# Order of the mixer's projections, gates and recurrence end in a two-layer block: attention's projection ahead of the recurrence's end, the inverse's matrices four turns behind their load

## The chip, the cores and the metric

The kernel runs on 1 core of one Trainium2 chip. The metric is the device time of one execution in microseconds, the median of several; lower is better. TensorE (PE) multiplies matrices, VectorE (DVE), ScalarE (ACT) and GpSimd (POOL) work elementwise, and SyncE (SP) issues the DMAs. Each engine carries out its own list of instructions in the order in which the program was built, and waits at an instruction until what that one needs is there.

## The reference, cut to what matters

Two layers (`DEPTH = 2`) over 256 tokens of width 1024, in float32. Each is a feed-forward block, a mixer and a second feed-forward block, all with norms before and behind and a residual.

```python
m = _mixer(h, w_in[l], rwkv_params, diff_params, w_branch[l], w_out[l], lambda_init)
x = x + _rms_norm(m, mix_norm_post[l])

def _mixer(h, w_in, rwkv_params, diff_params, w_branch, w_out, lambda_init):
    z = h @ w_in
    z_dsa, z_rwkv, z_diff, z_gate = jnp.split(z, GROUP_CUTS, axis=-1)
    y_a = _dsa_branch(z_dsa)                     # attention over the 64 best keys
    y_b = _rwkv7_branch(z_rwkv, *rwkv_params)    # a recurrence over the tokens
    y_c = _diff_branch(z_diff, *diff_params, lambda_init)   # differential attention
    branches = jnp.stack([y_a, y_b, y_c], axis=2)
    proj = jnp.einsum('blnc,ncd->blnd', branches, w_branch)
    gates = jax.nn.sigmoid(z_gate.reshape(B, L, N_BRANCH, D_MODEL))
    merged = jnp.sum(gates * proj, axis=2)
    return merged @ w_out
```

So three branches a, b and c (n = 0, 1, 2), each 512 wide, are projected to 1024, gated, summed and multiplied by `w_out`.

## The kernel before

**Large products.** Each weight matrix comes in raw tiles of 1 MB (`raw`, issued by SP at L201, two places), is split into a high part `wh` (ACT, a cast, L220) and a rest `wl` (DVE, and while `self.share` is on sometimes POOL, L220), and each 128x512 product is three matmuls (L229 to L231: `wh` with the low part of the data, `wh` with the high part, `wl` with the high part). There are four places for `wh`/`wl`; a pool `extra` opens more of them where other tiles have gone. A raw place is free when both splits have read it, and only then does SP issue the next load into it.

**The mixer** (L469 to L615) runs the large products of the weights `w_in` (queries, keys, values, gates), then three projections with `w_branch` (`proj_steps`, L576) and then `w_out`. Beside these stand three jobs, written as generators: `dsa` (branch a), `rwkv_in` with `rwkv_solve` and `rwkv` (branch b) and `diff` (branch c). Each step of a large product calls `tick()`, which advances the jobs by one `yield`. What a job issues is put in at high priority, but its PE instructions stand behind the large product's last matmul at that time; instructions of the other engines are not bound to that. A priority list then sets one order for each engine, at build time.

**The gates.** `gate_steps(n, h)` (L505) computes half h of gate n and copies it to a tile (L509). Gate 1 lies in the tiles `g1`, in the pool `tp`; half 0 of gate 0 lies in `g0`, in the place of a residual tile; the rest in the pool `ep`. Order: (1,0), (1,1), (0,0), (0,1), (2,1); (2,0) was computed earlier. The sigmoids of all gates (L599 to L601) come behind everything, and exponentials (L629, of the softmax) use another table of ACT functions.

**The recurrence.** `rwkv_solve` writes matrices to DRAM and reads them back in another layout (`d` L990 and L995, `zs` L992, `xs` L997), yields once (L1001), builds the matrices `Z` of an inverse from `zs` on DVE (L1004) and `T` from `xs` on POOL (L1008), and then runs a chain of small products (`Z,up`; `W,T`). `rwkv` ends with `yb` (L1176). The mixer drains this job (L564), closes the pools of the recurrence (`c1`, L565), opens the pool `gp` in their place (L566) and splits `yb` into `yh`, `yl` (L571 to L574).

**The end of the mixer.** Projection 1 (of `yb`), projection 0 (of `ya`, adds projection 1's gated result), then the pools `c2` (with `tp`) are closed and the pool `extra` with seven places is opened over them (L608, L609); projection 2 adds projection 0's result, its sum is transposed (L587), split into `mh`, `ml`, and multiplied by `w_out` together with it in one run of steps (L610 to L615). For the first 128 tokens (t = 0) `w_out` runs ahead of the second (t = 1). `post_norm` (squares L309, rstd L311 and L312, L367, L368), the next block's norm (L332) and the transposes of `xn` (L341) follow; then the feed-forward block starts with `hl`, `hh`.

Of the kernel before, what the change touches and what calls it, by code (L numbers as in the profile page):

```python
# [11 lines left out]
AF = mybir.ActivationFunctionType  # L12
# [11 lines left out]
LAG = 2  # L24
# [13 lines left out]
class Block:  # L38
# [430 lines left out]
    def mixer(self, l, ctx):  # L469
        nc, ins = self.nc, self.ins  # L470
# [7 lines left out]
        acc = lambda: self.bank(self.acc)  # L478
# [3 lines left out]
        def rows(c0):  # L482
            return lambda k0, k: w[k0 * 128:(k0 + k) * 128, c0:c0 + 512]
# [9 lines left out]
        gates, mx, kept = {}, {}, {}  # L493

        def gate(n, t, h):

            if n != 1 and (n, h) != (0, 0):
                return self.ep.tile([128, 512], F32, name="g", tag="s")
            key, o = (n, t if n == 1 else 0), h if n == 1 else t
            if not o:  # L500
                kept[key] = (self.tp.tile([128, 1024], F32, name="g1", tag="qk", bufs=4) if n == 1 else
                             self.xp.tile([128, 1024], F32, name="g0", tag="x0"))
            return kept[key][:, o * 512:o * 512 + 512]

        def gate_steps(n, h, acc=acc):  # L505
            def gate_done(t, ps):
                with self.pe():
                    gates[n, t, h] = gate(n, t, h)
                    nc.scalar.copy(gates[n, t, h], ps[0])  # L509

            return self.steps_b(rows(C_G + n * D + h * 512), 512, 8, self.hx, acc, gate_done)
# [11 lines left out]
        c1 = ExitStack()  # L523
# [15 lines left out]
            return d  # L539

        self.gp = None
        st = {}
        self.share = SHARE
        st["qi"] = cols(C_QI, "qi")
        raw = self.load_a(w, C_KI, 72)
# [6 lines left out]
        rwkv = self.rwkv_in(w, l, st)  # L552
# [5 lines left out]
            self.tick()  # L558
        st["dk"] = cols(C_DK, "dk")
        diff = self.start(self.diff(st, vd))  # L560
        for n, h in ((1, 0), (1, 1), (0, 0), (0, 1), (2, 1)):
            self.run_skew(gate_steps(n, h))
        self.share = 0
        self.drain(rwkv)  # L564
        c1.__exit__(None, None, None)  # L565
        self.gp = self.pool(ctx, "gp", side="right")  # L566

        def pieces(y):
            return lambda k, t: tuple(p[k // 2][:, k % 2, t * 128:t * 128 + 128] for p in y)

        yb = self.new_y(self.gp)  # L571
        with self.p1():
            for i in range(2):
                self.split_to(yb[0][i], yb[1][i], st["yb"][:, 2 * i:2 * i + 2, :])  # L574

        def proj_steps(n, y, prev=None, last=False, acc=acc):  # L576
            def proj_done(h):
# [17 lines left out]
                out += self.steps_b(src, 512, 4, pieces(y), acc, proj_done(h))  # L595
            return out

        self.drain(dsa, diff)
        with self.p1(), self.behind(self.exp):  # L599
            for g in gates.values():  # L600
                nc.scalar.activation(g, g, AF.Sigmoid)  # L601
        self.run_skew(proj_steps(1, yb))
        self.run_skew(proj_steps(0, st["ya"], prev=1))
        for t in range(2):
            self.x[t] = self.xp.tile([128, D], F32, name=f"xr{t}", tag=f"x{t}")
            nc.sync.dma_start(self.x[t], xd[t])
        gpost = self.bcast(ins["mix_norm_post"][l], D, self.gbp, "gb", "gpost")
        c2.__exit__(None, None, None)  # L608
        self.extra = self.pool(ctx, "extra", EXTRA)  # L609
        steps = proj_steps(2, st["yc"], prev=0, last=True, acc=self.wide)  # L610
        wo = ins["w_out"][l]
        steps += self.steps_b(lambda k0, k: wo[k0 * 128:(k0 + k) * 128, :], D, 8,
                              lambda k, t: tuple(p[:, k % 4, :] for p in mx[t, k // 4]), self.wide,
# [176 lines left out]
    def rwkv_in(self, w, l, st):  # L790

        nc = self.nc

        def shifted(dst, m0):
            raw = self.load_a(w, C_RW + m0 * 128, 256)
            ps = self.bank(self.acc)
            self.gemm_a(raw, 256, ps)
            with self.pe():
                for j in range(2):
                    z, p = dst[j], ps[:, j * T:(j + 1) * T]  # L800
                    nc.scalar.mul(z, p, self.omu[:, m0 + j:m0 + j + 1])
                    nc.vector.scalar_tensor_tensor(z[:, 1:T], p[:, 0:T - 1], self.mu[:, m0 + j:m0 + j + 1], z[:, 1:T],
                                                   op0=OP.mult, op1=OP.add)

        wa = self.rs.tile([128, T], F32, name="wa", bufs=1)
        sg = self.rs.tile([128, T], F32, name="sg", bufs=1)
        shifted([wa, sg], 12)
        strip = self.rs.tile([128, 16, 16], F32, name="strip", tag="q", bufs=8)
        halves = [dict(hf=hf, sg=sg) for hf in range(2)]
        self.start(self.rwkv_lora(halves, wa, sg))  # L810
        for hf, h in enumerate(halves):
            for n, m0 in (("k", 4), ("v", 8), ("r", 0)):
                d = self.ep.tile([128, 2, T], F32, name=n, tag="s")
                shifted([d[:, 0, :], d[:, 1, :]], m0 + 2 * hf)
                h[n] = d
            if hf == 0:
                self.start(self.rwkv_pre(h, strip))

        def job():
            yield from self.rwkv_pre(halves[1], strip)  # L820
            while "ready" not in halves[0]:
                yield
            Z = yield from self.rwkv_solve(list(zip(halves[0]["up"], halves[1]["up"])), strip)
            yield from self.rwkv(halves, Z, l, st)

        return self.start(job())

    def rwkv_lora(self, halves, wa, sg):
# [140 lines left out]
    def rwkv_solve(self, Ls, strip):  # L969

        nc = self.nc
# [26 lines left out]
        d16 = self.diag16.rearrange("p (b x) -> p b x", x=16)[:, None, :, :].to_broadcast([128, 4, 8, 16])  # L998
        even = self.even.rearrange("p b h x -> p (b h) x")[:, None].to_broadcast([128, 4, 8, 16])
        Zs, Ts = [], []  # L1000
        yield  # L1001
        for q in range(4):
            Zs.append(self.ep.tile([128, 4, 128], F32, name="Z", tag="s"))
            nc.vector.tensor_tensor(Zs[q].rearrange("p u (g x) -> p u g x", x=16),  # L1004
# [8 lines left out]
        for i, mask in enumerate(self.lev):  # L1013
# [23 lines left out]
            for g in range(2):  # L1037
                yield

                m = 64 if i == 2 else 128  # L1040
# [200 lines left out]
```

## Time and profile before

| | us |
|---|---|
| time, median of 3 runs (1476.93 to 1480.19) | 1479.91 |
| the profiled execution, device time | 1478.08 |
| its span in the profile | 1476.4 |
| PE busy (97% of the span) | 1430.3 |
| DVE busy (62%) | 910.1 |
| ACT busy (48%) | 707.7 |
| POOL busy (11%) | 166.5 |

PE is busy for all but 46 us of the span, so a change moves the time by what it adds to or takes from PE's idle time and PE's half clock; what other engines do counts where PE waits for it. The mixer of layer 0 ends at about 548 us of the span, that of layer 1 some 728 us later, with the same instructions. Idle times in square brackets in the rows are those of the row's engine just before the instruction, with what released it.

### The profile page before, as it was taken

The page shows a single profiled execution, that of the slowest core. Times are in us where ns is not written, and L with a number is a line of the kernel's source. Part 1 is how long each engine was busy: PE and PEld are TensorE (multiplying, and loading weights), DVE is VectorE, ACT ScalarE, POOL GpSimd, SP SyncE. Part 2 cuts the span into 40 slices and gives each one's busy share as a digit, 9 for nine tenths or more (in the row PEclk, how much of TensorE's full clock was granted, in tenths as well). Part 3 has the DMA queues.
Part 4 walks back from the last instruction along what each step waited for, and adds up shares of the span by engine and source line. Part 5 has one row for each costly group of instructions (what it writes and reads, how often), then busy time and mean ns, then how long its engine had stood idle before and what let it go on. Part 6 is the DMA issues. An engine that isn't in the chain of part 4 may idle for free.

```text
span 1476.4 us, 22534 instructions
## 1 busy us (share of the span) xinstructions
PE 1430.3 (97%) x9229; PEld 1277.5 (87%) x9229; DVE 910.1 (62%) x1312; ACT 707.7 (48%) x1086; POOL 166.5 (11%) x132
## 2 busy tenths in 40 slices
PE   8999999999799999999999999999889999999997
PEld 5999879988688778998889998799778888799986
DVE  5555463898655776555565554558976567755543
ACT  5444455555463454444454444455544544544442
POOL 1000011332212000000000000213421110000000
PEclk9999999999899999999999999999999999999999
DMA  6656656444433464665646556554442425555653
GB/s 219 194 173 206 208 201 183 141 143 130 119 97 104 157 229 143 191 194 188 226 144 190 182 200 230 169 172 149 139 130 89 141 87 205 179 171 173 209 176 113
DMA packets 176415, 247.05 MB, mean 167 GB/s; under 512 B 17908, under 2 KB 128440, under 8 KB 176312
## 3 DMA queue, kind: packets, MB, share of 16 engines
q1 hardware_dynamic: 176312, 245.62, 51.4%
q8 instruction: 72, 1.18, 0.3%
q14 instruction: 31, 0.25, 0.0%
HBM read 241.80 MB, written 3.80 MB: 166 GB/s over the span
## 4 chain that ended last, share of the span: by engine, by line
PE 78%; DVE 12%; DMA 4%; ACT 3%; issue 2%; POOL 0%; DVEq 0%; POOLq 0%; ACTq 0%; SPq 0%
PE ps L229 12%; PE ps L231 12%; PE ps L230 12%; PE ps L225 11%; PE ps L226 11%; PE ps L227 11%; PE ps L188 7%; DVE wl L220 3%; DMA raw<-in_w_out_dram 1%; ACT wh L220 1%; DVE sc L670 1%; PE ps L341 1%; DMA raw<-in_w_in_dram 1%; DVE sc L665 1%; DMA raw<-in_ffn_w_gate_dram 1%
## 5 line engine op out<-in xcount | busy, mean ns | idle before, releaser
L220 DVE TENSOR_TENSOR wl<-raw,wh 128x1024 fp32r<-128x1024 f32 x398 | 491.7, 1243 | 383.9 <-ACT wh L220 381.8
L220 ACT CAST wh<-raw 128x1024 fp32r<-128x1024 f32 x438 | 453.1, 1046 | 504.9 <-PE ps L226 232.0
L225 PE MATMUL ps<-hl,wh 128*128 128x256 f32 (+1 forms) x1712 | 488.9, 286 | 0.0
L226 PE MATMUL ps<-hh,wh 128*128 128x256 f32 (+1 forms) x1712 | 486.2, 284 | 0.0
L227 PE MATMUL ps<-hh,wl 128*128 128x256 f32 (+1 forms) x1712 | 486.0, 284 | 0.0
L225 PEld LDWEIGHTS ps<-hl,wh 128*128 128x128 f32 (+1 forms) x1712 | 327.0, 191 | 2.2 <-issue 1.3
L226 PEld LDWEIGHTS ps<-hh,wh 128*128 128x128 f32 (+1 forms) x1712 | 327.1, 191 | 0.4
L227 PEld LDWEIGHTS ps<-hh,wl 128*128 128x128 f32 (+1 forms) x1712 | 327.1, 191 | 0.0
L229 PE MATMUL ps<-wh,hl 128*128 128x512 f32 x384 | 161.0, 419 | 2.2 <-DVE hl L220 1.9
L231 PE MATMUL ps<-wl,hh 128*128 128x512 f32 x384 | 152.6, 398 | 2.4 <-DVE wl L220 2.4
L230 PE MATMUL ps<-wh,hh 128*128 128x512 f32 x384 | 151.6, 395 | 0.0
L229 PE MATMUL ps<-wh,gl 128*128 128x512 f32 x352 | 138.7, 394 | 0.0
L231 PE MATMUL ps<-wl,gh 128*128 128x512 f32 x352 | 138.4, 393 | 0.0
L230 PE MATMUL ps<-wh,gh 128*128 128x512 f32 x352 | 138.4, 393 | 0.0
L220 POOL TENSOR_TENSOR wl<-raw,wh 128x1024 fp32r<-128x1024 f32 x40 | 99.5, 2486 | 250.3 <-ACT wh L220 177.5
L312 POOL TENSOR_TENSOR rstd<-rstd,mhalf 128x1 f32<-128x1 f32 x24 | 20.2, 843 | 904.3 <-DVE rstd L311 904.3
L231 PEld LDWEIGHTS ps<-wl,hh 128*128 128x128 f32 x384 | 72.6, 189 | 22.1 <-DVE wl L220 5.1
L229 PEld LDWEIGHTS ps<-wh,hl 128*128 128x128 f32 x384 | 72.9, 190 | 20.1 <-issue 3.8
L230 PEld LDWEIGHTS ps<-wh,hh 128*128 128x128 f32 x384 | 73.0, 190 | 13.0
L231 PEld LDWEIGHTS ps<-wl,gh 128*128 128x128 f32 x352 | 66.0, 188 | 15.5
L230 PEld LDWEIGHTS ps<-wh,gh 128*128 128x128 f32 x352 | 66.0, 188 | 15.2
L229 PEld LDWEIGHTS ps<-wh,gl 128*128 128x128 f32 x352 | 66.0, 188 | 15.1
(267 smaller groups left out, 1481.2 us busy)
## 6 DMA issues: line engine op xcount, KB each, us to landing
raw<-in_w_in_dram SPq DMA_DIRECT2D x66, 1024.0 KB, 5.1
raw<-in_ffn_w_up_dram SPq DMA_DIRECT2D x44, 1024.0 KB, 5.3
raw<-in_ffn_w_down_dram SPq DMA_DIRECT2D x44, 1024.0 KB, 4.9
raw<-in_ffn_w_gate_dram SPq DMA_DIRECT2D x43, 1024.0 KB, 5.3
raw<-in_w_branch_dram SPq DMA_DIRECT2D x12, 1024.0 KB, 5.0
raw<-in_w_out_dram SPq DMA_DIRECT2D x8, 1024.0 KB, 5.8
gpre<-in_ffn_norm_pre_dram SPq DMA_DIRECT2D x4, 512.0 KB, 5.3
gpost<-in_ffn_norm_post_dram SPq DMA_DIRECT2D x4, 512.0 KB, 6.2
```

The costliest lines, as they stand in the source:

```text
L188: self.small = self.nc.tensor.matmul(*a, **k)
L220: return self.nc.scalar.copy(hi, src), (engine or self.nc.vector).tensor_sub(lo, src, hi.bitcast(F32))
L225: mm(ps, wh, xl, start=first, stop=False)
L226: mm(ps, wh, xh, start=False, stop=False)
L227: self.last = mm(ps, wl, xh, start=False, stop=last)
L229: mm(ps, xl, wh, start=first, stop=False)
L230: mm(ps, xh, wh, start=False, stop=False)
L231: self.last = mm(ps, xh, wl, start=False, stop=last)
L312: nc.gpsimd.tensor_tensor(r, r, self.mhalf[:, 0:1], op=OP.pow)
L341: self.tr = nc.tensor.transpose(ps[:, k, :], xns[h][:, k * 128:(k + 1) * 128], self.ident)
L665: nc.vector.scalar_tensor_tensor(sc, rl[:, j, :], wi[:, t, head:head + 1], src, op0=OP.mult, op1=OP.add)
L670: nc.vector.match_replace(sc, m8, sc, USED)
```

## The change

Two things change, each in both layers.

First, the mixer's order. Gates come as (0,0), (0,1), (1,0), (1,1), (2,1); the sigmoids of gate 0 are issued after (1,0), those of gates 1 and 2 behind the recurrence's end. Projection 0 (of `ya`) stands ahead of that end and adds nothing; the recurrence's own job calls `close()`, which closes its pools, opens `gp` and splits `yb`. Then projection 1 adds projection 0's result, and projection 2 adds projection 1's, so that the `g1` tiles in the pool `tp` are read until projection 2's last addition, while the pool `extra` is opened over them as before.

Second, `rwkv_solve` yields 2 * LAG = 4 times instead of once between the loads `zs`, `xs` and the building of `Z` and `T`.

```diff
--- before.py
+++ after.py
@@ -539,7 +539,16 @@
             return d
 
         self.gp = None
-        st = {}
+
+        def close():
+
+            c1.__exit__(None, None, None)
+            self.gp = self.pool(ctx, "gp", side="right")
+            y = st["ybs"] = self.new_y(self.gp)
+            for i in range(2):
+                self.split_to(y[0][i], y[1][i], st["yb"][:, 2 * i:2 * i + 2, :])
+
+        st = {"close": close}
         self.share = SHARE
         st["qi"] = cols(C_QI, "qi")
         raw = self.load_a(w, C_KI, 72)
@@ -558,20 +567,8 @@
             self.tick()
         st["dk"] = cols(C_DK, "dk")
         diff = self.start(self.diff(st, vd))
-        for n, h in ((1, 0), (1, 1), (0, 0), (0, 1), (2, 1)):
-            self.run_skew(gate_steps(n, h))
-        self.share = 0
-        self.drain(rwkv)
-        c1.__exit__(None, None, None)
-        self.gp = self.pool(ctx, "gp", side="right")
-
         def pieces(y):
             return lambda k, t: tuple(p[k // 2][:, k % 2, t * 128:t * 128 + 128] for p in y)
-
-        yb = self.new_y(self.gp)
-        with self.p1():
-            for i in range(2):
-                self.split_to(yb[0][i], yb[1][i], st["yb"][:, 2 * i:2 * i + 2, :])
 
         def proj_steps(n, y, prev=None, last=False, acc=acc):
             def proj_done(h):
@@ -595,19 +592,31 @@
                 out += self.steps_b(src, 512, 4, pieces(y), acc, proj_done(h))
             return out
 
+        def open_gates(n):
+            for (m, t, h), g in gates.items():
+                if m == n:
+                    nc.scalar.activation(g, g, AF.Sigmoid)
+
+        for n, h in ((0, 0), (0, 1), (1, 0), (1, 1), (2, 1)):
+            self.run_skew(gate_steps(n, h))
+            if (n, h) == (1, 0):
+                with self.p1():
+                    open_gates(0)
+        self.run_skew(proj_steps(0, st["ya"]))
+        self.share = 0
+        self.drain(rwkv)
+        with self.p1(), self.behind(self.exp):
+            for n in (1, 2):
+                open_gates(n)
+        self.run_skew(proj_steps(1, st["ybs"], prev=0))
         self.drain(dsa, diff)
-        with self.p1(), self.behind(self.exp):
-            for g in gates.values():
-                nc.scalar.activation(g, g, AF.Sigmoid)
-        self.run_skew(proj_steps(1, yb))
-        self.run_skew(proj_steps(0, st["ya"], prev=1))
         for t in range(2):
             self.x[t] = self.xp.tile([128, D], F32, name=f"xr{t}", tag=f"x{t}")
             nc.sync.dma_start(self.x[t], xd[t])
         gpost = self.bcast(ins["mix_norm_post"][l], D, self.gbp, "gb", "gpost")
         c2.__exit__(None, None, None)
         self.extra = self.pool(ctx, "extra", EXTRA)
-        steps = proj_steps(2, st["yc"], prev=0, last=True, acc=self.wide)
+        steps = proj_steps(2, st["yc"], prev=1, last=True, acc=self.wide)
         wo = ins["w_out"][l]
         steps += self.steps_b(lambda k0, k: wo[k0 * 128:(k0 + k) * 128, :], D, 8,
                               lambda k, t: tuple(p[:, k % 4, :] for p in mx[t, k // 4]), self.wide,
@@ -822,6 +831,7 @@
                 yield
             Z = yield from self.rwkv_solve(list(zip(halves[0]["up"], halves[1]["up"])), strip)
             yield from self.rwkv(halves, Z, l, st)
+            st["close"]()
 
         return self.start(job())
 
@@ -998,7 +1008,8 @@
         d16 = self.diag16.rearrange("p (b x) -> p b x", x=16)[:, None, :, :].to_broadcast([128, 4, 8, 16])
         even = self.even.rearrange("p b h x -> p (b h) x")[:, None].to_broadcast([128, 4, 8, 16])
         Zs, Ts = [], []
-        yield
+        for _ in range(2 * LAG):
+            yield
         for q in range(4):
             Zs.append(self.ep.tile([128, 4, 128], F32, name="Z", tag="s"))
             nc.vector.tensor_tensor(Zs[q].rearrange("p u (g x) -> p u g x", x=16),
```

What this does to the order of the engines' instructions, in layer 0 (layer 1 reads alike). In a row, `wl<-raw,wh` is the second split of a weight, `yl<-ps,yh` that of `ya` or `yc`, and a wait for a DMAHW queue is one for a transfer.

**DVE, where `Z` is built.** Before:

```order
L988 COPY XT<-X 128x256 [waits DVE_49]
L220 TENSOR_TENSOR wl<-raw,wh 128x1024 [waits DMAHW1_49,PE_49,Activation_49]
L220 TENSOR_TENSOR yl<-ps,yh 128x512 [waits Activation_49]
L1004 TENSOR_TENSOR Z<-zs,blk_1947 128x512 [waits DMAHW5_49]
L1004 TENSOR_TENSOR Z<-zs,blk_1947 128x512 x2
L220 TENSOR_TENSOR wl<-raw,wh 128x1024 [waits DMAHW2_49,PE_49,Activation_49]
L220 TENSOR_TENSOR yl<-ps,yh 128x512 [waits Activation_49]
L1004 TENSOR_TENSOR Z<-zs,blk_1947 128x512
```

After:

```order
L998 COPY XT<-X 128x256 [waits DVE_49]
L220 TENSOR_TENSOR wl<-raw,wh 128x1024 [waits DMAHW1_49,PE_49,Activation_49]
L220 TENSOR_TENSOR yl<-ps,yh 128x512 [waits Activation_49]
L1015 TENSOR_TENSOR Z<-zs,blk_1947 128x512 [waits DMAHW5_49]
L1015 TENSOR_TENSOR Z<-zs,blk_1947 128x512 x2
L220 TENSOR_TENSOR wl<-raw,wh 128x1024 [waits DMAHW2_49,PE_49,Activation_49]
L220 TENSOR_TENSOR yl<-ps,yh 128x512 [waits Activation_49]
L1015 TENSOR_TENSOR Z<-zs,blk_1947 128x512
```

Nothing moved: three of the four `Z` stand ahead of the same `wl` and the same `yl` (the split of `ya`, which empties the PSUM bank that the next product `dk,dq` on PE is written to). What moved is PE's `Z,up`, from 6 matmuls behind the products `dk,dq` to 28 behind.

**PE, at the recurrence's end** (`yc` and `yt` are its last transposes; L229 with `yl` opens a projection). Before:

```order
L191 MATMUL ps<-ident,yc 128x128 [waits DVE_49]
L191 MATMUL ps<-ident,yc 128x128 x2
L191 MATMUL ps<-ident,yt 128x128 x8
L229 MATMUL ps<-wh,yl 128x512 [waits DVE_49]
L230 MATMUL ps<-wh,yh 128x512 [waits Activation_49]
L231 MATMUL ps<-wl,yh 128x512
```

After:

```order
L229 MATMUL ps<-wh,yl 128x512 [waits Activation_49]
L230 MATMUL ps<-wh,yh 128x512
L231 MATMUL ps<-wl,yh 128x512
...
L191 MATMUL ps<-ident,yc 128x128 [waits DVE_49,PE_49]
L191 MATMUL ps<-ident,yc 128x128 [waits DVE_49]
L191 MATMUL ps<-ident,yc 128x128 x2
L229 MATMUL ps<-wh,yl 128x512
```

Projection 0's matmuls now stand ahead of, between and behind these transposes; the last four `yt` are followed by 97 large matmuls before the next small one.

**ACT, around the softmax** (L629, after L638, is the exponential, L601, after L598, the sigmoid). Before:

```order
L629 ACTIVATE lm,smd<-lm,nmd 128x256 x4
L601 ACT_TABLE_LOAD
L601 ACTIVATE g<-g 128x512
L220 CAST wh<-raw 128x1024
L601 ACTIVATE g<-g 128x512
```

After:

```order
L598 ACT_TABLE_LOAD
L598 ACTIVATE g<-g 128x512
...
L598 ACTIVATE g<-g 128x512
L1073 COPY bk<-ps 128x512
L638 ACT_TABLE_LOAD
L638 ACTIVATE lm,smd<-lm,nmd 128x256 x4
L1073 COPY bk<-ps 128x512
L598 ACT_TABLE_LOAD
L598 ACTIVATE g<-g 128x512
```

Sigmoids now stand between groups of exponentials: per layer seven loads of a table (four for L598, three for L638) in place of one for L601, 22 in the program in place of 10.

**DVE, at `w_out`** (L581 and L583, after L578 and L580, multiply a gate by a projection and add the one before). Before:

```order
L220 TENSOR_TENSOR wl<-raw,wh 128x1024 [waits DMAHW4_49,Activation_49]
L220 TENSOR_TENSOR wl<-raw,wh 128x1024 [waits Activation_49]
L220 TENSOR_TENSOR ml<-ps,mh 128x512 [waits Activation_49] x2
L581 TENSOR_TENSOR g<-g,ps 128x512 [waits PE_49]
L220 TENSOR_TENSOR wl<-raw,wh 128x1024 [waits DMAHW5_49,Activation_49]
L220 TENSOR_TENSOR wl<-raw,wh 128x1024 [waits Activation_49]
L583 TENSOR_TENSOR g<-g 128x512 [waits DVE_49]
L581 TENSOR_TENSOR g<-g,ps 128x512 [waits PE_49]
L583 TENSOR_TENSOR g<-g 128x512 [waits DVE_49]
```

After:

```order
L220 TENSOR_TENSOR ml<-ps,mh 128x512 [waits Activation_49] x2
L578 TENSOR_TENSOR g<-g,ps 128x512 [waits PE_49]
L580 TENSOR_TENSOR g<-g,g_4401 128x512 [waits DVE_49]
L578 TENSOR_TENSOR g<-g,ps 128x512 [waits PE_49]
L580 TENSOR_TENSOR g<-g,g_4416 128x512 [waits DVE_49]
L220 TENSOR_TENSOR ml<-ps,mh 128x512 [waits Activation_49]
L220 TENSOR_TENSOR wl<-raw,wh 128x1024 [waits Activation_49]
L220 TENSOR_TENSOR wl<-raw,wh 128x1024 [waits DMAHW5_49,Activation_49]
L220 TENSOR_TENSOR wl<-raw,wh 128x1024 [waits Activation_49]
```

The splits of `w_out`'s second tile onward moved behind the last additions.

**PE, at the end of `w_out`.** Before:

```order
L231 MATMUL ps<-wl,mh 128x512
L341 MATMUL ps<-ident,xn 128x128 [waits DVE_49,PE_49]
L341 MATMUL ps<-ident,xn 128x128 x3
L229 MATMUL ps<-wh,ml 128x512
L341 MATMUL ps<-ident,xn 128x128 [waits DVE_49,PE_49]
L341 MATMUL ps<-ident,xn 128x128 x3
L230 MATMUL ps<-wh,mh 128x512
L231 MATMUL ps<-wl,mh 128x512
```

After:

```order
L231 MATMUL ps<-wl,mh 128x512
L341 MATMUL ps<-ident,xn 128x128 [waits DVE_49,PE_49]
L341 MATMUL ps<-ident,xn 128x128 x3
L341 MATMUL ps<-ident,xn 128x128 [waits DVE_49,PE_49]
L341 MATMUL ps<-ident,xn 128x128 x3
L229 MATMUL ps<-wh,hl 128x512 [waits DVE_49]
L230 MATMUL ps<-wh,hh 128x512 [waits Activation_49]
```

Six matmuls of `w_out` stood among and behind the transposes; now all stand ahead, and of t = 1's 48 matmuls 29 are left behind t = 0's last one, where there were 39.

## Rows read from the trace of the kernel before

**Rows 1.** The page: busy time, share of the span and instructions of PE, and the chain of work that ended last, by engine.

```profile
PE 1430.3 (97%) x9229; PEld 1277.5 (87%) x9229; DVE 910.1 (62%) x1312; ACT 707.7 (48%) x1086; POOL 166.5 (11%) x132
...
PE 78%; DVE 12%; DMA 4%; ACT 3%; issue 2%; POOL 0%; DVEq 0%; POOLq 0%; ACTq 0%; SPq 0%
```

**Rows 2.** Busy time by stretch of the span: the stretch, its us, then busy time and instructions of PE, PEld, DVE, ACT and POOL, TensorE's granted clock, the share of the DMA engines, GB/s.

```profile
380.00:400.00 20.00, 19.24 (x111) 16.40 (x112) 13.14 (x29) 9.68 (x28) 2.39 (x1) 0.86 0.33 106
400.00:420.00 20.00, 19.33 (x120) 16.47 (x119) 12.77 (x27) 9.51 (x29) 3.41 (x2) 1.00 0.33 104
440.00:460.00 20.00, 19.99 (x118) 17.03 (x117) 11.68 (x31) 8.88 (x19) 5.61 (x4) 1.00 0.40 132
460.00:480.00 20.00, 20.00 (x130) 17.80 (x128) 8.92 (x19) 7.08 (x12) 3.50 (x2) 1.00 0.30 106
495.00:540.00 45.00, 45.00 (x204) 36.46 (x203) 36.23 (x43) 20.63 (x23) 0.00 (x0) 1.00 0.65 221
1218.00:1222.00 4.00, 4.00 (x12) 3.14 (x11) 2.02 (x5) 1.12 (x4) 0.00 (x0) 0.57 0.93 356
```

**Rows 3.** Timeline of DVE in layer 0 about the building of `Z`: start, us, engine, line, operation, how many, idle time before and its releaser.

```profile
364.19 1.22 DVE L220 TENSOR_TENSOR wl<-raw,wh 128x1024 fp32r<-128x1024 f32 x1
372.78 4.02 DVE L1004 TENSOR_TENSOR Z<-zs,blk 128x512 f32<-128x512 f32 x3 [6.77 <-DMA zs<-d]
376.71 3.36 DVE L220 TENSOR_TENSOR wl<-raw,wh 128x1024 fp32r<-128x1024 f32 x1
380.00 0.68 DVE L220 TENSOR_TENSOR yl<-ps,yh 128x512 fp32r<-128x512 f32 x1
```

**Rows 4.** Timeline of SP's queue in the same place.

```profile
369.27 0.37 SPq L992 DMA_DIRECT2D zs<-d  x1
...
370.91 9.61 SPq L201 DMA_DIRECT2D raw<-in_w_in_dram  x2
```

**Rows 5.** Timeline of PE, the first products of `dk` and `dq`, in layer 0 and in layer 1.

```profile
380.73 1.22 PE L188 MATMUL ps<-dk,dq 64*128 64x128 f32 x6 [8.22 <-DVE yl L220]
...
1107.10 1.22 PE L188 MATMUL ps<-dk,dq 64*128 64x128 f32 x6 [7.17 <-DVE yl L220]
```

**Rows 6.** Busy time by stretch just behind these two places (columns as in group 2).

```profile
380.70:385.40 4.70, 4.67 (x16) 3.87 (x17) 3.15 (x5) 1.18 (x6) 0.00 (x0) 0.50 0.70 223
1107.10:1112.50 5.40, 5.40 (x21) 4.60 (x21) 3.12 (x5) 1.26 (x6) 0.00 (x0) 0.50 0.59 194
```

**Rows 7.** Timeline of PE, ACT and DVE at the start of projection 1 in layer 0, and PE's first matmul of it in layer 1.

```profile
488.06 1.04 PE L191 MATMUL ps<-ident,yt 128*128 128x128 f32 x8
...
489.50 0.63 ACT L220 CAST yh<-yb 128x512 fp32r<-128x512 f32 x1
...
490.16 0.69 DVE L220 TENSOR_TENSOR yl<-yb,yh 128x512 fp32r<-128x512 f32 x1 [0.26 <-ACT yh L220]
...
490.90 0.50 PE L229 MATMUL ps<-wh,yl 128*128 128x512 f32 x1 [1.80 <-DVE yl L220]
...
491.93 0.39 PE L230 MATMUL ps<-wh,yh 128*128 128x512 f32 x1
...
493.29 0.39 PE L230 MATMUL ps<-wh,yh 128*128 128x512 f32 x1
...
1217.61 0.50 PE L229 MATMUL ps<-wh,yl 128*128 128x512 f32 x1 [1.80 <-DVE yl L220]
```

**Rows 8.** Timeline of ACT, DVE and PE from the end of `w_out` for t = 0 to the transposes of `xn` in layer 0, DVE's last addition of projection 2, and PE's `xn` in layer 1.

```profile
529.38 0.69 DVE L583 TENSOR_TENSOR g<-g 128x512 f32<-128x512 f32 x1
...
539.62 0.59 ACT L309 ACTIVATE junk<-ps 128x512 bf16<-128x512 f32 x1
...
540.20 1.03 ACT L220 CAST wh<-raw 128x1024 fp32r<-128x1024 f32 x1
...
545.38 0.63 ACT L309 ACTIVATE junk<-xr 128x512 bf16<-128x512 f32 x1 [3.56 <-issue]
...
543.28 1.41 DVE L367 SCALAR_TENSOR_TENSOR xn<-ps,rstd,gpost 128x512 f32<-128x512 f32 x2 [0.67 <-POOL rstd L312]
...
549.96 0.69 DVE L220 TENSOR_TENSOR hl<-ps,hh 128x512 fp32r<-128x512 f32 x1 [0.77 <-ACT hh L220]
...
548.68 0.63 PE L341 MATMUL ps<-ident,xn 128*128 128x128 f32 x4 [1.48 <-DVE xn L332]
...
1277.35 0.63 PE L341 MATMUL ps<-ident,xn 128*128 128x128 f32 x4 [0.97 <-DVE xn L332]
```

**Rows 9.** Timeline of SP's queue about `w_out`, and the page's row on the time from issue to landing.

```profile
524.11 0.37 SPq L201 DMA_DIRECT2D raw<-in_w_out_dram  x1
...
528.17 5.20 SPq L201 DMA_DIRECT2D raw<-in_ffn_w_gate_dram  x2
...
raw<-in_w_out_dram SPq DMA_DIRECT2D x8, 1024.0 KB, 5.8
```

**Rows 10.** Loads of a table of ACT functions: the group of L601 over the whole span (busy, mean ns), and the timeline of ACT about the one in layer 0.

```profile
L601 ACT ACT_TABLE_LOAD x2 | 2.6, 1283 | 0.0
...
430.97 0.18 ACT L629 ACTIVATION_READ_ACCUMULATOR lm<-lm,nmd 128x1 f32 x1
431.17 1.28 ACT L601 ACT_TABLE_LOAD   x1
432.46 0.63 ACT L601 ACTIVATE g<-g 128x512 f32<-128x512 f32 x1
```

## The prediction

> **What bounds the kernel now.** I read the page first: PE is busy for 1430.3 of 1476.4 us and holds 78% of the chain that ended last [rows 1]. So time comes from PE's 46 idle microseconds and from its stretches at half clock, and an edit elsewhere counts only if it makes PE wait or spares it a wait. I then went through the windows for those in which PE isn't full, and through PE's timeline for what released it. Three places are touched by the change.
>
> The first is the building of `Z`. SP issues the load `zs` at 369.27; DVE stands idle for 6.77 us, builds three `Z` from 372.78 on, and only then splits a weight (376.71) and `ya` (380.00), which stand behind `Z` in its list [rows 3, 4]. PE waits 8.22 us for that last split, and 7.17 us in layer 1 [rows 5]. Behind both waits PE runs at a granted clock of 0.50 (1.2 GHz), for 4.7 and 5.4 us [rows 6]; work done at half clock takes twice as long, so this adds about 2.3 and 2.7 us. The two places cost 8.2 + 7.2 + 2.3 + 2.7 = 20.4 us together.
>
> The second is the start of projection 1. It needs the split of `yb`, which the recurrence delivers last: PE has done its transposes by 489.1, then ACT copies and casts, DVE splits, and PE starts at 490.90 after 1.80 us idle; the same 1.80 us in layer 1 [rows 7]. In layer 1 a stretch at a mean clock of 0.57 follows: of 4 us, 4 × 0.43 = 1.7 us are lost [rows 2].
>
> The third is the end of the mixer. From the square of `w_out`'s result for t = 0 (539.62) to the transposes of `xn` (548.68) a chain over ACT, POOL and DVE takes 9.06 us; PE covers most of it with `w_out`'s matmuls for t = 1 and waits 1.48 us, 0.97 in layer 1 [rows 8].
>
> **The change part by part.**
>
> *The four turns.* They move nothing on DVE. The order of its list is the same before and after: three `Z`, which wait for `zs`, ahead of the same weight split and the same split of `ya`. What is put off are PE's products `Z,up`, and PE did not wait for these here; it waited for `ya`'s split. So the 20.4 us stay: 0 us. The reason is in the code too: a yield binds PE's instructions to PE's large products, no other engine's.
>
> *Projection 0 ahead of the recurrence's end.* PE now has projection 0's matmuls between and behind the last transposes, 97 large ones behind the last four. At 0.227 us each ((493.29 − 491.93) / 6, [rows 7]) that is 22 us beside a chain of copy, cast and split of under 3 us. The 1.80 us go, in both layers: −3.6. With the wait in layer 1 I let its half clock go too, less some doubt: −1.5 (between −1.7 and 0). Sum −5.1. Projection 0 itself needs `ya`, which was split at 380.00, long before, so nothing is late in its stead.
>
> *Sigmoids between exponentials.* ACT now loads a table seven times per layer instead of once, six more at 1.283 us [rows 10]: 7.7 us of ACT per layer, 15.4 in all. ACT is busy 9.5 of 20 us there [rows 2], so ACT as such has room. But each load of the exponentials' table stands right ahead of a softmax, on which jobs of PE hang. The bounds: nothing, if large products always cover it (PE is full from 440 to 480, 39.99 of 40 us, but not at 380 to 420, where it lacks 0.76 and 0.67 [rows 2]), or all 15.4. The list of PE shows the recurrence's small products closer together than before in that stretch, so cover is thinner. I take one load per layer as exposed, +2.6, since most stand where PE was full.
>
> The Trainium skill (ScalarE: Activation LUTs, What ACT_TABLE_LOAD costs) says that a switch of table costs 1283 ns and a drain of about 1380 ns more. In this trace the load starts 0.02 us behind the end of the instruction before it and the next one starts 0.01 us behind the load [rows 10]; no drain shows. By the skill's price one exposed load per layer would be 5.3 us as an estimate, not 2.6.
>
> *The end of the mixer.* Projection 2's last additions now read `g1` in the pool `tp`, and the places of `extra`, into which `w_out`'s splits go, lie over it. In DVE's list all splits of `w_out` from the second tile on now follow the last additions; before, four of them stood ahead. In the trace the fourth raw tile of `w_out` is issued at 524.11, ahead of the last addition at 529.38, and the feed-forward's first at 528.17 [rows 8, 9]. Now I count from the end T of projection 2's matmuls (additions 0.69 us each, casts 1.03, splits 1.22, [rows 3, 8]): the first split behind the additions ends at about T + 4, and frees the place of the third tile; the fourth follows at T + 6.3. Each takes about 5.8 us to land [rows 9]: T + 10 and T + 12. PE has 40 matmuls and 8 transposes (some 0.6 us for four, [rows 8]) ahead of the third tile's first, 9.1 + 1.2 = 10.3 us, so the tiles come in time or up to 0.6 us late: +0.3. Then four prices:
> - PE's list puts 19 of t = 1's 48 matmuls ahead, to fill while the tiles are late; 29 are left to cover the chain to `xn` where 33 were left ahead of it (and six beside and behind it): 4 × 0.227 = +0.9.
> - The feed-forward's casts and splits come later too and now stand within that chain (a cast of 1.03 between the two squares, a split or two of 1.22 ahead of rstd, partly beside one another): +1.5.
> - Behind the transposes of `xn` nothing of `w_out` is left, so that cast and split of `hh`, `hl` show: from the transposes at 548.68 `hl` needed until 550.65 [rows 8], less the second four transposes: +1.0.
> - The tiles: +0.3.
>
> That is +3.7 per layer, +7.4 in all. Bounds: if the casts slip beside the chain and half of `hl` is covered, 0.9 + 0.5 per layer, +2.8; if each layer also gets a stretch at half clock like that of 1218 (1.7) and the tiles are 0.6 late, 3.7 + 1.7 + 0.3 = 5.7 each, +11.4.
>
> *The rest* (gates in another order, `gp` opened by the job, a residual's load a little earlier) leaves the number of matmuls as it is and changes no wait that I found: 0.
>
> **The sum**, against the profiled execution's 1478.08: 0 − 5.1 + 2.6 + 7.4 = +4.9, which gives 1483.0. That run lies 1.8 below the median of the runs shown; on the median, 1479.91 + 4.9 = **1484.8 us**. About 0.2%, 3 us, is what a measurement of this kernel can tell from no change.
>
> **The rivals.**
> - *A. The end of the mixer is covered.* The late tiles come in time and the casts fit beside the chain: +2.8, and no table load shows: −5.1 + 2.8 = −2.3, 1477.6; with a tail as good as before −5.1, 1474.8. For it: PE is full from 495 to 540 now [rows 2], and DVE and ACT have room. Against it: a wait of 1.48 shows already with more cover.
> - *B. `Z` does give way.* If the list of DVE let the two splits go ahead, PE would start `dk,dq` at about 373.6, some 7 us earlier, and the half clock would go: up to 9.4 per layer, 1484.8 − 19 = 1466. The order speaks against it outright; this would need a wait that I read wrongly.
> - *C. The middle loses more.* The recurrence's small products, closer together, wait one after another for ACT (tables) and DVE: three loads per layer exposed in place of one, +5.1, and the half clock behind a long wait, 1.7 or 2.5 per layer: +9, so 1494. It decides from the point where the large products between two links of that chain take less than the link's 2 to 3 us, some ten matmuls.
> - *D. The change's parts cancel*: the gain at projection 1 and the loss at the end are of one size, 1478 to 1483; this is my forecast with its terms a third smaller.
>
> **How the numbers follow.** My forecast, loss over 0.2%, 0.37; C 0.13; D 0.25; A 0.21; B 0.04. Faster by over 0.2% are B and most of A: 0.22. Within 0.2% are D and the rest of A: 0.28. Slower by over 0.2%: 0.50. The range holds A's better end and C: 1474.5 to 1494; B and a middle worse than C are left out. The likeliest case alone, slower, lies between 1483 and 1490.
>
> **What would show it.** In the profile after, DVE's idle time ahead of the first `Z` should be there still, 6 to 7 us, and PE's wait for `dk,dq` 7 to 8 us, at half clock. PE's wait at projection 1's start should be gone. PE should wait some 3 to 4 us ahead of `xn` and about 1 us ahead of the feed-forward's first `hl`, in both layers, and `w_out`'s last two tiles should be issued behind the last addition. In ACT's rows 12 more table loads of 1.28 us should stand. The prediction fails if PE's wait at `dk,dq` shrinks (B), if the wait ahead of `xn` stays at 1.5 (A), or if windows between 380 and 490 show PE short by more than 4 us in a layer (C).

## The result, and the profile after

The changed kernel is slower: 1497.38 us (median of 4, 1495.46 to 1497.87) against 1480.05 for the kernel before, a ratio of 1.0119 with an interval of 1.0101 to 1.0136. The sign was forecast, the size wasn't: 17.3 us in place of 4.9, and the time lies above the range that was given. The span of the profiled execution grew by 19.5 us, from 1476.4 to 1495.9.

PE's busy time on the page is 15.4 us longer than in [rows 1], though it has as many matmuls:

```profile
PE 1445.7 (97%) x9229; PEld 1284.8 (86%) x9229; DVE 913.9 (61%) x1310; ACT 724.3 (48%) x1098; POOL 172.7 (12%) x134
```

Busy time grows with the same work where the clock is halved (four products `ar,bk` take 1.10 us at full clock and 2.07 at half, below). So beside PE's waits the stretches at half clock have to be sought out; the windows below do that.

**What stayed.** DVE still waits for `zs` ahead of the first `Z`, and PE still waits for the split behind it, in both layers (DVE's and PE's timelines; the counterparts are [rows 3] and [rows 5]):

```profile
372.86 4.03 DVE L1015 TENSOR_TENSOR Z<-zs,blk 128x512 f32<-128x512 f32 x3 [6.66 <-DMA zs<-d]
...
380.83 1.22 PE L188 MATMUL ps<-dk,dq 64*128 64x128 f32 x6 [6.95 <-DVE yl L220]
...
1119.02 1.22 PE L188 MATMUL ps<-dk,dq 64*128 64x128 f32 x6 [6.82 <-DVE yl L220]
```

**What went.** At the recurrence's end PE goes from the last transposes straight into projections, with no idle time in brackets where [rows 7] had 1.80 us (PE's timeline, layer 0; layer 1 has no wait there either):

```profile
501.90 0.60 PE L191 MATMUL ps<-ident,yt 128*128 128x128 f32 x4
502.26 0.48 PE L229 MATMUL ps<-wh,yl 128*128 128x512 f32 x1
```

**What came at the end of the mixer.** PE's waits ahead of `xn` and ahead of the feed-forward's first matmul, in layer 0 and layer 1; then DVE's last addition of projection 2, ACT with a cast between the two squares, and SP's queue (the counterparts are [rows 8] and [rows 9]):

```profile
557.51 1.94 PE L341 MATMUL ps<-ident,xn 128*128 128x128 f32 x8 [2.61 <-DVE xn L332]
560.00 0.79 PE L229 MATMUL ps<-wh,hl 128*128 128x512 f32 x1 [0.55 <-DVE hl L220]
...
1295.28 1.29 PE L341 MATMUL ps<-ident,xn 128*128 128x128 f32 x8 [2.62 <-DVE xn L332]
1297.70 0.70 PE L229 MATMUL ps<-wh,hl 128*128 128x512 f32 x1 [1.14 <-DVE hl L220]
...
532.20 0.69 DVE L580 TENSOR_TENSOR g<-g,g 128x512 f32<-128x512 f32 x1
...
552.12 0.63 ACT L309 ACTIVATE junk<-xr 128x512 bf16<-128x512 f32 x1 [0.86 <-ACT wh L220]
...
552.75 1.04 ACT L220 CAST wh<-raw 128x1024 fp32r<-128x1024 f32 x1
...
553.69 0.63 ACT L309 ACTIVATE junk<-xr 128x512 bf16<-128x512 f32 x1
...
521.90 15.90 SPq L201 DMA_DIRECT2D raw<-in_w_out_dram  x3
...
543.51 0.37 SPq L201 DMA_DIRECT2D raw<-in_ffn_w_gate_dram  x1
```

The row at 521.90 holds `w_out`'s last three tiles: the first goes out there, the last by 537.8, behind the last addition (532.20); before, the last went out at 524.11, 5 us ahead of it. PE waits 2.61 us ahead of `xn` and 0.55 ahead of the feed-forward in layer 0, 2.62 and 1.14 in layer 1; before, it waited 1.48 and 0.97 us ahead of `xn` and not at all ahead of the feed-forward.

**What came in the middle.** Here is what the forecast had at nothing. PE's timeline at the recurrence's second group of products `ar,bk`, DVE's and GpSimd's beside it, in layer 0 (layer 1 reads alike, 737.8 us later), and behind them PE's and DVE's rows of the kernel before at the same products:

```profile
462.20 1.10 PE L188 MATMUL ps<-ar,bk 64*128 64x256 f32 x4 [0.56 <-DVE yc L1162]
...
466.15 1.13 PE L188 MATMUL ps<-ar,bk 64*128 64x256 f32 x4 [1.74 <-DVE lk L1104]
...
467.64 1.37 PE L188 MATMUL ps<-ar,bk 64*128 64x256 f32 x4
...
469.67 2.07 PE L188 MATMUL ps<-ar,bk 64*128 64x256 f32 x4
...
462.42 2.62 DVE L1170 TENSOR_TENSOR yc<-yc,ln 128x256 f32<-128x256 f32 x1
...
465.42 0.68 DVE L1104 TENSOR_TENSOR lk<-ps,mT 128x512 f32<-128x512 f32 x1
...
462.39 2.37 POOL L220 TENSOR_TENSOR wl<-raw,wh 128x1024 fp32r<-128x1024 f32 x1 [1.13 <-ACT wh L220]
```

```profile
456.78 1.82 PE L188 MATMUL ps<-ar,bk 64*128 64x256 f32 x8
...
458.96 1.83 PE L188 MATMUL ps<-ar,bk 64*128 64x256 f32 x8
...
455.87 0.42 DVE L1159 TENSOR_TENSOR yc<-yc,ln 128x256 f32<-128x256 f32 x1
...
457.91 0.69 DVE L1093 TENSOR_TENSOR lk<-ps,mT 128x512 f32<-128x512 f32 x1 [0.17 <-PE ps L188]
```

PE waits 0.56 us, then 1.74 us for `lk`, a mask that DVE applies; before, these products ran without a wait. DVE applies the mask late because a step of the recurrence's normalisation (`yc<-yc,ln`) ahead of it took 2.62 us where it took 0.42; it ended 0.3 us behind the weight split that GpSimd began at 462.39. Then four products `ar,bk` take 2.07 us where four took 1.10, and the clock, by window, is at half:

```profile
386.50:461.00 74.50, 74.48 (x470) 62.55 (x469) 41.90 (x86) 49.25 (x107) 12.36 (x7) 1.00 0.35 114
1123.80:1198.70 74.90, 74.85 (x472) 62.88 (x471) 41.90 (x86) 49.25 (x107) 12.31 (x7) 1.00 0.35 113
468.40:475.20 6.80, 6.80 (x19) 4.50 (x17) 3.68 (x9) 1.96 (x3) 0.00 (x0) 0.50 0.00 0
1205.70:1212.50 6.80, 6.80 (x16) 4.23 (x16) 3.83 (x8) 1.45 (x3) 0.09 (x1) 0.50 0.00 0
557.10:564.00 6.90, 5.94 (x18) 4.71 (x19) 6.90 (x11) 3.78 (x6) 1.46 (x1) 0.51 0.80 282
1297.80:1301.30 3.50, 3.50 (x9) 2.73 (x10) 3.50 (x6) 2.62 (x4) 0.00 (x0) 0.51 0.88 280
```

The third figure from the right is the granted clock: 0.50 (1.2 GHz) in the stretches at 468 and at 1206, right behind PE's waits, and 0.51 at the ends of the two mixers. 6.8 us at half clock cost 3.4 us. From 386.5 to 461, where all seven table loads of layer 0's mixer for gates and softmaxes lie, PE is busy for 74.48 of 74.50 us at full clock, and for 74.85 of 74.90 us where those of layer 1 lie (1123.8 to 1198.7).

### The profile page after: what moved, and what is told of

Same layout as the page of the kernel before. It is cut to its first block, busy times and chain, and to the rows that moved or that the text cites. A ratio compares the mean times of both kernels' runs of the same rounds, so it can differ in the third digit from the quotient of the medians.

```text
span 1495.9 us, 22549 instructions
## 1 busy us (share of the span) xinstructions
PE 1445.7 (97%) x9229; PEld 1284.8 (86%) x9229; DVE 913.9 (61%) x1310; ACT 724.3 (48%) x1098; POOL 172.7 (12%) x134
## 5 line engine op out<-in xcount | busy, mean ns | idle before, releaser
L229 PE MATMUL ps<-wh,hl 128*128 128x512 f32 x384 | 164.3, 428 | 3.9 <-DVE hl L220 3.6
L231 PE MATMUL ps<-wl,hh 128*128 128x512 f32 x384 | 156.2, 408 | 2.4 <-DVE wl L220 2.4
L230 PE MATMUL ps<-wh,hh 128*128 128x512 f32 x384 | 156.1, 407 | 0.0
L229 PE MATMUL ps<-wh,gl 128*128 128x512 f32 x352 | 138.8, 394 | 0.0
L220 POOL TENSOR_TENSOR wl<-raw,wh 128x1024 fp32r<-128x1024 f32 x42 | 104.3, 2482 | 256.1 <-ACT wh L220 153.9
L229 PEld LDWEIGHTS ps<-wh,hl 128*128 128x128 f32 x384 | 75.4, 196 | 21.7 <-DVE hl L220 4.7
L230 PEld LDWEIGHTS ps<-wh,hh 128*128 128x128 f32 x384 | 75.3, 196 | 16.3 <-issue 2.6
L229 PEld LDWEIGHTS ps<-wh,gl 128*128 128x128 f32 x352 | 66.0, 188 | 15.1
```

Of the source, the lines that this page charges most:

```text
L220: return self.nc.scalar.copy(hi, src), (engine or self.nc.vector).tensor_sub(lo, src, hi.bitcast(F32))
L229: mm(ps, xl, wh, start=first, stop=False)
L230: mm(ps, xh, wh, start=False, stop=False)
L231: self.last = mm(ps, xh, wl, start=False, stop=last)
```

## The experiments

The median of the kernel before is 1475.57 to 1480.05 us in the four sets of runs, so each kernel is told as a ratio to the kernel before in the same set; 0.001 is 1.5 us. The changed kernel stands at 1.0119. Each ratio has an interval of some 0.002 to either side, so a difference of two ratios is good to about 4 us.

### One turn again

```diff
-        for _ in range(2 * LAG):
-            yield
+        yield
```

> The changed kernel with the single yield ahead of Z put back; the mixer's new order stays. Theory 1 (the four turns bring the recurrence's chain to a place where DVE reaches the products' masks lk late): PE's waits and half clock at the second ar,bk group go, some 6 to 7 us per layer, so 1497.4 - 13 = about 1484 to 1486. Theory 2 (the tables and the gates' new order make that loss): they stay, 1496 to 1498. In both the wait at dk,dq and the waits ahead of xn stay.

Measured: 1484.84 us, 1.0059 (1.0038 to 1.0080), so 0.0060 or 9 us of the 17 were the turns' (13 were expected). Both groups `ar,bk` run without a wait, and PE is full (PE's timeline):

```profile
455.69 1.82 PE L188 MATMUL ps<-ar,bk 64*128 64x256 f32 x8
...
457.87 1.84 PE L188 MATMUL ps<-ar,bk 64*128 64x256 f32 x8
```

And 30 us about that place by window (columns as in [rows 2]):

```profile
440.00:470.00 30.00, 29.99 (x181) 25.78 (x180) 15.52 (x39) 12.49 (x23) 7.98 (x5) 1.00 0.29 94
```

Theory 1 holds; what is left above the kernel before is about what the end of the mixer costs, below. PE's wait at `dk,dq` was to stay; it is 6.89 us in layer 1, but 4.52 in layer 0, where the next two runs on the changed kernel, with four turns, have 4.62 and 4.35. So that drop is not the turns'.

### The turns alone, on the kernel before

```diff
-        yield
+        for _ in range(2 * LAG):
+            yield
```

> The kernel before with four yields instead of one, nothing else. Theory 1: the loss at the second ar,bk group appears here, and the 1.80 us at projection 1 stay: 1480 + 10 to 13 = 1490 to 1493. Theory 2: 1479 to 1482. DVE's idle time ahead of the first Z stays at 6 to 7 us in both.

Measured: 1500.41 us, 1.0163 (1.0144 to 1.0183), worse than the whole change and than either theory said. The loss at `ar,bk` is there (waits of 0.56 and 1.72 us, half clock at 466.5), which speaks for theory 1; what theory 1 had not seen is a second wait, at the recurrence's last transposes, 3.95 us and half clock again (PE's timeline):

```profile
498.33 0.90 PE L191 MATMUL ps<-ident,yc 128*128 128x128 f32 x3 [3.95 <-DVE yc L1166]
```

And its stretches by window:

```profile
466.50:473.30 6.80, 6.80 (x19) 4.40 (x17) 3.59 (x9) 1.83 (x4) 0.00 (x0) 0.50 0.00 0
497.20:504.10 6.90, 5.56 (x18) 4.58 (x19) 3.72 (x9) 2.87 (x7) 0.00 (x0) 0.51 0.62 230
```

Put off by the turns, the recurrence ends when the gates' products have run out: no large product is left ahead of the transposes to fill PE's wait. In the changed kernel projection 0 stands there. So the order of the projections is worth much where the turns are, and the two halves of the change are not independent.

### The split that GpSimd ran beside the normalisation

```diff
+            pooled = self.share and self.splits % self.share == 0
+            self.pooled += bool(pooled)
-            pair = self.split_to(hi, lo, src, self.nc.gpsimd if self.share and self.splits % self.share == 0 else None)
+            pair = self.split_to(hi, lo, src, self.nc.gpsimd if pooled and self.pooled % 21 != 20 else None)
```

> The changed kernel, but one weight split per layer, the one that GpSimd runs at 462.39 beside DVE's yc chain, is done by DVE. If DVE's yc row of 2.62 us is long because GpSimd's split runs beside it, it falls to 0.4, lk comes some 1 to 2 us earlier, PE's wait of 1.74 shrinks below 0.7 and the half clock behind it (3.4 us) goes: 1497.4 - 2 x 4 to 5 = 1487 to 1490. If the order of DVE's list alone is the cause, the waits stay within 0.5 us and the time is 1495 to 1498.

Measured: 1486.07 us, 1.0070 (1.0046 to 1.0093): 7 us less than the changed kernel, for one split in each layer. The normalisation's step is back at 0.42 us, `lk` follows although DVE now does the split itself, and PE waits 0.57 and 0.54 us (DVE's and PE's timelines):

```profile
458.92 0.42 DVE L1172 TENSOR_TENSOR yc<-yc,ln 128x256 f32<-128x256 f32 x1
...
459.72 1.22 DVE L222 TENSOR_TENSOR wl<-raw,wh 128x1024 fp32r<-128x1024 f32 x1
460.85 0.68 DVE L1106 TENSOR_TENSOR lk<-ps,mT 128x512 f32<-128x512 f32 x1
...
458.70 1.10 PE L188 MATMUL ps<-ar,bk 64*128 64x256 f32 x4 [0.57 <-DVE yc L1164]
...
462.01 1.36 PE L188 MATMUL ps<-ar,bk 64*128 64x256 f32 x8
...
464.58 1.13 PE L188 MATMUL ps<-ar,bk 64*128 64x256 f32 x4 [0.54 <-DVE lk L1106]
```

No half clock follows these shorter waits (the granted clock is 1.00 from 440 to 480). So the turns brought the recurrence to a bad place, and GpSimd's split made a wait of half a microsecond there into one of 1.7 us with a stretch at half clock behind it.

### Projection 1's sum kept in projection 0's tiles

```diff
-                        if prev is not None:
+                        if prev is not None and last:
                             nc.vector.tensor_add(g, g, gates[prev, t, h])
+                        elif prev is not None:
+                            nc.vector.tensor_add(gates[prev, t, h], gates[prev, t, h], g)
...
-        steps = proj_steps(2, st["yc"], prev=1, last=True, acc=self.wide)
+        steps = proj_steps(2, st["yc"], prev=0, last=True, acc=self.wide)
```

> The changed kernel, but projection 1 adds its result into projection 0's tiles, so that projection 2 reads those and the g1 tiles under the extra places are free before it. If the late splits of w_out cost what was predicted (3.7 per layer), the waits ahead of xn go back to 1.0 to 1.5 us and the half clock there goes: 1497.4 - 7 to 8 = 1489 to 1491. If they are due to something else, such as the feed-forward's casts, 1496 to 1498.

Measured: 1485.75 us, 1.0072 (1.0049 to 1.0096), 7 us less than the changed kernel. The waits ahead of `xn` are those of the kernel before again, and the feed-forward's first matmul does not wait (PE's timeline, layer 0 and 1):

```profile
553.25 0.63 PE L341 MATMUL ps<-ident,xn 128*128 128x128 f32 x4 [1.62 <-DVE xn L332]
...
1284.64 0.63 PE L341 MATMUL ps<-ident,xn 128*128 128x128 f32 x4 [0.93 <-DVE xn L332]
```

So the late splits were the cause, at 7 us for an expected 7 to 8.

### The order alone, and two mends with the turns

Both have the edit above. The first has this beside it, the second the edit of the split on DVE:

```diff
-        for _ in range(2 * LAG):
-            yield
+        yield
```

> The changed kernel with the single yield put back and projection 1's sum kept in projection 0's tiles, so of the change only the new order of gates and projections is left. If turns and late splits are all that the change lost, PE's wait at projection 1's start (1.80 per layer) is gone and nothing stands in its place: 2 to 5 us under the kernel before. If the tables or the gates' order cost something of their own, it ends at the kernel before or up to 4 us above it.

> The changed kernel with two causes taken out: projection 1's sum kept in projection 0's tiles, and the one weight split per layer that GpSimd ran beside DVE's yc chain done by DVE; the four turns stay. If the two losses add up (7 us each by the runs that mended one), it comes to the kernel before, within 4 us. If mending one only hands the wait on to the next, it stays 6 us or more above.

Measured: 0.9996 (0.9978 to 1.0015) and 1.0005 (0.9988 to 1.0021), 10 runs each. The two losses add up: with both mended the changed kernel is the kernel before again. The order alone ends there too, and not 2 to 5 us under it: it meets the second case of its expectation, in which the tables or the gates' order cost something of their own, though no row here shows such a cost. PE's wait of 1.80 is gone in its trace (0.28 and 0.29 us are left, at the transposes of `yc`). The interval of the order alone runs from 3.3 us under the kernel before to 2.2 above. So the -5.1 that was forecast for projection 0 isn't there in the time, and how much of the 3.6 us of waits was given back isn't shown.

### `Z` on GpSimd

```diff
-            nc.vector.tensor_tensor(Zs[q].rearrange("p u (g x) -> p u g x", x=16),
+            nc.gpsimd.tensor_tensor(Zs[q].rearrange("p u (g x) -> p u g x", x=16),
```

> The kernel before with the four Z built by GpSimd instead of DVE, so that DVE's weight split and the split of ya no longer stand behind the load of zs. If that order is what makes PE wait at dk,dq, the wait falls from 8.2 and 7.2 to under 2 us and its half clock goes: up to 15 to 20 us faster, less what Z loses by GpSimd's longer list (four times 1.5 us, and a weight split behind it), so 1463 to 1473. If PE waits for the transfers themselves, the wait stays above 5 us and the time within 4 us of the kernel before.

Measured on the kernel before: 1468.15 us, 0.9926 (0.9902 to 0.9951). DVE's splits no longer stand behind `zs`, and PE's wait of 8.22 us at `dk,dq` is gone; smaller ones for `Z` are left (DVE's and PE's timelines, layer 0):

```profile
370.91 1.23 DVE L220 TENSOR_TENSOR wl<-raw,wh 128x1024 fp32r<-128x1024 f32 x1 [3.99 <-ACT wh L220]
372.05 0.68 DVE L220 TENSOR_TENSOR yl<-ps,yh 128x512 fp32r<-128x512 f32 x1
...
374.11 0.72 PE L188 MATMUL ps<-dk,dq 64*128 64x128 f32 x8
...
376.25 0.60 PE L188 MATMUL ps<-Z,up 128*128 128x128 f32 x4
...
377.41 0.71 PE L188 MATMUL ps<-Z,up 128*128 128x128 f32 x4 [0.55 <-POOL Z L1004]
```

So the order of DVE's list was the cause of the wait that the four turns were put behind, and these could not touch it. The gain, 11 us of the 20 that the place cost, is what the expected time allowed for.

> The changed kernel as it is, with the four Z built by GpSimd. If the wait at dk,dq and the loss at the second ar,bk group are separate, it gains about 8 us on the changed kernel: 1.2% above the kernel before becomes 0.6% above. If the four turns hurt only because the chain starts late, an earlier Z doesn't help there, since the turns still set when PE takes Z,up: the waits of 0.7 and 1.7 at ar,bk stay.

The same edit on the changed kernel: 1504.84 us, 1.0170 (1.0149 to 1.0191), not a gain at all. The second half of the expectation holds, the waits at `ar,bk` stay (0.57 and 1.70 us). The first fails: PE runs on through `dk,dq` and then waits 4.31 us for a weight split that stands behind the `Z` on GpSimd (PE's, GpSimd's and DVE's timelines):

```profile
385.36 0.79 PE L231 MATMUL ps<-wl,hh 128*128 128x512 f32 x1 [4.31 <-POOL wl L220]
...
378.52 4.48 POOL L1015 TENSOR_TENSOR Z<-zs,blk 128x512 f32<-128x512 f32 x2
382.96 2.34 POOL L220 TENSOR_TENSOR wl<-raw,wh 128x1024 fp32r<-128x1024 f32 x1
...
382.63 2.76 DVE L756 TENSOR_SCALAR lm<-lm,smd,lam 128x128 f32<-128x128 f32 x2
```

> The new order of gates and projections, with the single yield, projection 1's sum in projection 0's tiles, and the four Z built by GpSimd. If the gains add up, the 8 us of the Z built by GpSimd and the 3.6 us of projection 1's wait: 10 to 12 us under the kernel before. If the earlier Z chain only lets the recurrence reach another crowded place, 4 to 8 us under it.

The order, the sum in projection 0's tiles, one turn and `Z` on GpSimd: 1469.54 us, 0.9930 (0.9914 to 0.9946). It beats both kernels. Its 10 us are the number of the first case, but not by its sum: `Z` on GpSimd alone gave 11 where 8 were reckoned with, and the order alone nothing that shows (0.9996), so it adds nothing here either.

### No table between the softmaxes

```diff
-                    nc.scalar.activation(g, g, AF.Sigmoid)
+                    nc.scalar.activation(g, g, AF.Exp if n == 0 else AF.Sigmoid)
```

> The changed kernel, but gate 0 takes an exponential instead of a sigmoid, which leaves that part of the computation changed and no load of a table between the softmaxes: 12 loads of 1.28 us fewer. If the loads cost PE what was predicted (one per layer exposed), 2 to 3 us less than the changed kernel; if they are hidden, within 2 us of it; if they cost as rival C has it, 5 us or more less.

Measured: 1503.36 us, 1.0158 (1.0127 to 1.0188), none of the three. The edit also changed the order of PE's, DVE's and ACT's lists, so it isn't the test that it was meant to be: PE now waits at the first group `ar,bk` too (PE's timeline):

```profile
431.93 1.31 PE L188 MATMUL ps<-ar,bk 64*128 64x128 f32 x11 [1.98 <-DVE mb L1089]
```

What the loads cost is read from the changed kernel's own trace instead. They are there, 14 where [rows 10] had two (busy us, mean ns):

```profile
L598 ACT ACT_TABLE_LOAD x8 | 10.3, 1283 | 0.1
...
L638 ACT ACT_TABLE_LOAD x6 | 7.7, 1283 | 0.1
```

and PE is full where they lie, from 386.5 to 461 and from 1123.8 to 1198.7 (windows above). There they cost nothing. The changed kernel with the two mends has all 14 loads as well and takes the time of the kernel before.

## Why the prediction was wrong, step by step

| step | predicted | in the profile, both layers |
|---|---|---|
| four turns | 0 | +11.4, and 9 us by the run that took them back |
| projection 0 ahead of the end | -5.1 | -3.6 of waits, and no half clock of 1218 |
| table loads | +2.6 | 0 |
| end of the mixer | +7.4 | +9.2, and 7 us by the run that mended it |
| `Z` behind `zs` | stays | stays: 6.95 and 6.82 for 8.22 and 7.17 |

**The step that failed** is "They move nothing on DVE ... So the 20.4 us stay: 0 us." Its first half is right: the list of DVE around `Z` didn't move and PE's wait stayed. The 0 doesn't follow. The turns put off PE's `Z,up` and with it the whole chain of the recurrence, which the prediction itself noted as moved (28 matmuls behind `dk,dq` in place of 6): PE's first `Z,up` comes at 391.22 in place of 384.60. A chain that starts 6 us later meets other neighbours: at its second group `ar,bk` DVE has the normalisation of the group before ahead of `lk`, and GpSimd a weight split beside it. From the rows: (0.56 + 1.74 + 3.4) x 2 = 11.4 us. One turn takes away 9 of them and moving the split alone 7, so this is shown. With 11.4 in place of 0 the forecast's sum would be 16.3, for 17.3 measured. That it comes so near is in part luck: the tables were put 2.6 too high and the end of the mixer 1.8 too low.

**Rival C** had the place (the recurrence's small products, waiting link after link), the engine (DVE, beside ACT) and the half clock behind the wait, and 1494 for it. It was given 0.13, and half of a cause: it was hung on ACT's tables as much as on DVE, and not on the turns. The range ended at its time, with nothing for the end of the mixer at its upper bound beside it. Its sign, PE short by more than 4 us between 380 and 490, did not come: PE is short by 3.2 us there, since at half clock it counts as busy.

**The tables** were taken as exposed once per layer, by choice between 0 and 15.4; the trace shows 0. ACT had room, as its rows said. By the Trainium skill (ScalarE: Activation LUTs, What ACT_TABLE_LOAD costs) a switch costs a drain of about 1380 ns on top of its 1283; this case's rows have the 1283 alone, with 0.02 us ahead of the load and 0.01 behind it [rows 10].

**The end of the mixer** was right in mechanism, and in size within 2 us: the late tiles, the cast between the squares and the uncovered `hl` are all in the rows. (The +1.0 for `hl` doesn't come out of its own rows: 550.65 - 548.68 less 0.6 is 1.4; 0.55 and 1.14 were measured.) Of the end's 9.2, the waits are (2.61 + 0.55 - 1.48) + (2.62 + 1.14 - 0.97) = 4.5, and the half clock, of which 5.9 and 3.5 busy microseconds stood in the windows, (5.9 + 3.5) / 2 = 4.7; the forecast had the half clock in its upper bound alone.

**Projection 0** was right in what it does to PE: the waits of 1.80 went, in both layers. That the time came back isn't shown: the order alone measured 0.9996, and its interval leaves out -5.1.

**What stays open.** The waits and the half clock named here add up to 11.4 - 3.6 - 1.7 + 9.2 - 1.6 = 13.7 of the span's 19.5 us (the -1.6 are the shorter waits at `dk,dq`). Of the rest, 1.7 are a stretch at half clock in layer 1, from 1076.0 to 1079.4, ahead of `Z`, where both kernels have the same order. The changed kernel has two such stretches there; the kernel before and the one with the turns alone have one. Most of what is left is PE busy for longer at full clock: PE's busy time inside all stretches at half clock is 43.6 us for 20.3, and half of that difference, 11.7, leaves 3.7 of the 15.4 us by which its busy time grew. No run here says where they come from. What the order alone is worth without the turns was not resolved.

## What to carry to other kernels

A step that is put off costs nothing only if all that hangs on it is still covered where it lands: follow the chain that it starts to its end, engine by engine, and look at each place for what now stands ahead and what runs beside it, above all vector work beside GpSimd. Where a scheduler fixes the order of each engine, look whether an edit moves the instruction that waits; a yield that binds one engine doesn't move another engine's. And a tile that is read longer keeps closed the place that a prefetch was to use: let the sum stay in the tile whose place nobody needs.

## What the runs showed of the hardware

A DVE operation with two inputs in SBUF that began beside a weight split on GpSimd ended only behind that split: `yc<-yc,ln` took 2.62 us in place of 0.42. In the changed kernel with `Z` on GpSimd, `lm<-lm,smd`, a tensor with scalars, took 2.76 us for two in place of 0.60. `Z` itself, which has two such inputs, took 0.67 us at the least and 1.75 at the most in the kernel before, the longer ones beside GpSimd's `T`. The Trainium skill (GPSIMD Engine Reference, Specifications) says that the two engines share interfaces to SBUF, with contention for DVE instructions with two SBUF inputs or in a 2-port mode. The trace agrees for the two inputs (2.62 us for 0.42); whether `lm<-lm,smd` runs in a 2-port mode no run here shows. With the split taken off GpSimd at two such meetings the changed kernel was 7 us faster.

PE's waits of 0.57 and 0.54 us, some 5 us apart, were not followed by half clock; those of 0.56 and 1.74 at the same place were, for 6.8 us, so that waits of 2.3 us cost 5.7. The 1.80 us of [rows 7] were followed by it in one layer and not in the other.
